# One transformer layer: memory keys started ahead of the delta-rule scans, cross attention's sums in other PSUM banks, one activation table moved

## The chip, the core and the metric

The kernel runs on one core of a Trainium2 chip. The core has a matrix engine (TensorE, PE in the profile, with its weight loads as PEld), a vector engine (VectorE, DVE), an activation engine (ScalarE, ACT), a general engine (GpSimd, POOL) and a queue engine (SyncE, SP) that issues nearly all transfers here. Matrix results land in eight PSUM banks of 128 x 512 float32. The metric is the device time of one execution in microseconds (us), the median of several runs.

## What is computed

One layer over 1024 tokens of width 1024, batch 1:

```python
h = rms_norm(x, g_mix_pre);  proj = h @ w_in           # queries, keys, values of both mixers, gates, alpha, beta
attn_o = window_attention(rope(aq), rope(ak), av)      # 8 heads, +-128 tokens
dn_o = gated_deltanet(dqkv, dgate, dalpha, dbeta)      # 4 heads, forward and backward scan over chunks
x = x + rms_norm(concat(attn_o, dn_o) @ w_out)
c = cross_attention(rms_norm(x), rms_norm(mem), w_cq, w_ckv, w_co)   # 256 memory tokens, 4 heads of 256
x = x + rms_norm(c)
f = (silu(h @ w_gate) * (h @ w_up)) @ w_down;  x = x + rms_norm(f)
```

All is float32. The kernel gets its accuracy from split operands: each operand of a dense product is stored as a rounded part `hi` and a rest `lo` (both of a faster float32 form), and a product is the three matmuls hi·hi, hi·lo and lo·hi. The split is a ScalarE cast (line 102) and a VectorE subtraction (line 103), for weights 128 x 1024 at a time.

## The kernel before

The program is written with pools of tiles, and a scheduler orders the instructions of each engine, guided by its own model of time; the source order, priorities and the pools' places decide what it may do. Each engine then runs its list strictly in that order. A tile of a pool that is closed leaves its place (in SBUF, or a PSUM bank) to the next pool on the same side, and the new tile's first writer waits for the old tile's readers.

The stages: input projections with the short convolutions and the preparation of the delta rule (to about 300 us); attention projections, the inverses' last levels (`levels`), and the window attention, which goes on in pieces (`next_windows`, two at a time) until 568 us; the two scans (`scan(0)`, `scan(1)`, each for two heads and both directions, 8 steps) interleaved with the memory's keys and values; the output projection (`mid_gemm`, tiles pmg); cross attention; its output projection; the feed-forward network.

What the change touches:

- `ORDER_3` (line 38) sets the source order of the scan stage: `M` is `memory_norm` (squares of the memory tokens into mjk and mss, scaling of mt, 16 transposes ptm, the split into mT), `s01` one step of both scans, `W` two windows, `K` one of 8 blocks of keys (`next_keys`, weights w_ckv, 24 matmuls pck of 128x256), `V` one of two halves of the values (`next_values`, 48 matmuls pcv of 128x512).
- PSUM pool `pc` with 5 banks serves the scans' products (psc) and also ptm, pck and pcv. The window attention has its 3 banks (psw/ptw and pow).
- The pool `mk` (mT and the small tiles of the memory) lies on the left side, where the tiles of `levels` were.
- `load_w` loads a weight block into one of two buffers wraw; the two memory tiles mt take the same two buffers. Its transfers, as all others, are issued by SP in the order of its list.
- The step of a scan: pk = k·S (psc), R = v − …, pv, vg and vn, the new state S, then po and pq, whose sum is the output o; from step 4 on also the output's normalisation, with transposes (line 870) and a store to `d_mix` (line 875). The output projection loads `d_mix` again (mraw, line 1067).
- `cross_attention` (line 1100 on): scores pcs in the two banks of `px`, exponentials cpr, transposes pct, the split cph/cpl, and the weighted sums pco, before in the same two banks of `px`. `cross_q` makes the queries pcq in the four banks of `pg`.
- Line 1151 runs a Silu on a small tile, so that the table of that function is loaded ahead of the feed-forward stage.

Of the kernel before, what the change touches and what calls it, by code (L numbers as in the profile page):

```python
# [10 lines left out]
F32 = mybir.dt.float32  # L11
F32R = mybir.dt.float32r
I32 = mybir.dt.int32
AF = mybir.ActivationFunctionType
ALU = mybir.AluOpType
AX = mybir.AxisListType
PSUM = bass.MemoryType.PSUM
DRAM = bass.MemoryType.DRAM

P = 128  # L20
S = 1024
D = 1024
KT = D // P
# [6 lines left out]
ML = 256  # L30
# [4 lines left out]

ORDER_1 = "D0 P0 D1 P1 D2 B0 P2 D3 P3 B1".split()
ORDER_2 = "L0 L1 G0 G1 A4 V A0 A1 L2 L3 W W W A2 A3 G2 G3 W".split()
ORDER_3 = ("M " + "s01 W K " * 5 + "s01 K " * 3 + "s01 V V").split()


_NAMES = ["ident", "mUi", "mLi", "m5", "m6", "band0", "band1", "band2", "mU", "mL", "ones"]
# [34 lines left out]
def tile_hybrid_block(  # L76
# [6 lines left out]
    nc = tc.nc  # L83
# [9 lines left out]
    def f32(ap):  # L93
        return ap.bitcast(F32)
# [13 lines left out]
    def pool(name, bufs, **kw):  # L108
        return tc.tile_pool(name=name, bufs=bufs, reuse_waits="tile", **kw)
# [42 lines left out]
    pcv = ExitStack()  # L152
# [41 lines left out]
    pg = pgs.enter_context(pool("pg", 3, space=PSUM))  # L194
# [18 lines left out]
    for hf in range(2):  # L213
        hi = hx.tile([P, KT, HALF], F32R, name=f"hhi{hf}")
        lo = hx.tile([P, KT, HALF], F32R, name=f"hlo{hf}")
        for j in range(4):
# [5 lines left out]
            ss = t1.tile([P, 1], F32, tag="ss", name="ss", bufs=4)  # L222
# [4 lines left out]
            for kq in range(2):  # L227
                pt = small()
# [15 lines left out]
    pt = small()  # L244
# [75 lines left out]
    pt = small()  # L320
# [42 lines left out]
    pt = small()  # L363
# [403 lines left out]


    p2 = ExitStack()
    pc = p2.enter_context(pool("pc", 5, space=PSUM))  # L770
    t3 = p2.enter_context(pool("t3", 2, side="right"))

    def scan(g):
# [106 lines left out]
        yield  # L880


    mk = p2.enter_context(pool("mk", 1))
    mT = [mk.tile([P, KT, ML], F32R, name=f"mT{i}") for i in range(2)]

    def memory_norm():
        mn = []
        for t in range(2):
            mt = wp.tile([P, D], F32, tag="wraw", name="mt")
            nc.sync.dma_start(mt, mem[t * P:(t + 1) * P, :])  # L890
            jk = f32(wp.tile([P, D], F32R, tag="whi", name="mjk"))
            ss = mk.tile([P, 1], F32, tag="mss", name="mss", bufs=2)
            nc.scalar.activation(jk, mt, AF.Square, accum_out=ss)
            rs = mk.tile([P, 1], F32, tag="mrs", name="mrs", bufs=2)
            rstd_of(rs, ss, 1.0 / D, EPS)
            nc.vector.tensor_scalar(mt, mt, rs, None, ALU.mult)
            mn.append(mt)
        for k2 in range(KT // 2):
            pt = pc.tile([P, 2, ML], F32, tag="pc", name="ptm")
            for i in range(2):  # L900
                k = 2 * k2 + i
                for j in range(2):
                    nc.tensor.transpose(pt[:, i, j * P:(j + 1) * P], mn[j][:, k * P:(k + 1) * P], ident)
            for i in range(2):
                k = 2 * k2 + i
                split(mT[0][:, k, :], mT[1][:, k, :], pt[:, i], gain("mem", k))
# [3 lines left out]
    def next_keys():  # L910

        ct = kv_done[0]
        kv_done[0] += 1
        whi, wlo = load_w(w_ckv[:, ct * P:(ct + 1) * P], KT, P)
        pp = pc.tile([P, 512], F32, tag="pc", name="pck")[:, 0:ML]
        for k in range(KT):
            for i, (w, a) in enumerate(((whi, 0), (whi, 1), (wlo, 0))):
                nc.tensor.matmul(pp, w[:, k, :], mT[a][:, k, :], start=(k == 0 and i == 0), stop=(k == KT - 1 and i == 2))
        cv = mk.tile([P, 512], F32, tag="cv", name="cv", bufs=2)[:, 0:ML]
        nc.scalar.copy(cv, pp)  # L920
        nc.sync.dma_start(d_mk[ct * P:(ct + 1) * P, :], cv)

    def next_values():

        ch = kv_done[1]
        kv_done[1] += 1
        pp = [pc.tile([P, 512], F32, tag="pc", name="pcv") for _ in range(2)]
        for kp in range(4):
            whi, wlo = load_w(w_ckv[kp * 256:(kp + 1) * 256, D + ch * 512:D + (ch + 1) * 512], 2, 512)
            for t in range(2):  # L930
                for kk in range(2):
                    k = 2 * kp + kk
                    for i, (w, a) in enumerate(((whi, 0), (whi, 1), (wlo, 0))):
                        nc.tensor.matmul(pp[t], mT[a][:, k, t * P:(t + 1) * P], w[:, kk, :], start=(k == 0 and i == 0),
                                         stop=(k == KT - 1 and i == 2))
        for t in range(2):
            vv = mk.tile([P, 512], F32, tag="cv", name="vv", bufs=2)
            nc.scalar.copy(vv, pp[t])
            nc.sync.dma_start(d_mv[t, :, ch * 512:(ch + 1) * 512], vv)
# [159 lines left out]
    def cross_attention(q, h):  # L1099
# [29 lines left out]
            split(ph, pl, pt)  # L1129
            pts.append((ph, pl))  # L1130
        for j in range(2):
            po = px.tile([P, 512], F32, tag="px", name="pco")
            cs = slice((2 * h + j) * P, (2 * h + j + 1) * P)
            for kt in range(2):
                for i, (a, b_) in enumerate(((0, 0), (0, 1), (1, 0))):
                    nc.tensor.matmul(po, vr_[a][:, kt, cs], pts[kt][b_], start=(kt == 0 and i == 0),  # L1136
                                     stop=(kt == 1 and i == 2))
            split(q[0][:, 2 * h + j, :], q[1][:, 2 * h + j, :], po)
# [9 lines left out]
            behind = q, h  # L1148
    q1 = q
    last = cross_attention(*behind)  # L1150
    nc.scalar.activation(last, last, AF.Silu)
    L2.close()
    Lk.close()

# [386 lines left out]
```

## Time and profile before

| | us |
|---|---|
| three runs | 1549.28, 1548.82, 1545.64 |
| median | 1548.82 |
| profiled execution | 1551.7 |
| its span, first to last instruction | 1549.9 |

| stretch of the span, us | what runs | PE busy | DVE busy | granted PE clock |
|---|---|---|---|---|
| 362.8 to 389.5 | levels' end, memory norm, first scan step | 21.82 of 26.70 | 18.57 | 0.87 |
| 389.5 to 497.2 | six scan steps, keys, windows | 102.58 of 107.70 | 95.23 | 0.98 |
| 497.2 to 533.2 | last steps, keys | 33.59 of 36.00 | 31.76 | 0.96 |
| 533.2 to 568.4 | values, windows | 32.98 of 35.20 | 22.00 | 0.94 |
| 568.4 to 640 | output projection | 71.00 of 71.60 | 42.58 | 1.00 |
| 640 to 847 | cross attention, its output projection | 207.00 of 207.00 | 96.95 | 1.00 |
| 847 to 890 | last two heads, output projection | 39.70 of 43.00 | 16.24 | 0.96 |

How to read the rows below: a row of the timeline has the start and the duration in us, the engine, the line of the kernel, the operation, output<-input tiles, shapes, how many instructions are merged (xN), and in brackets the idle time before it with what ended it. A matmul's duration includes its pipeline, so the pace of a row of matmuls is read from one start to the next. A 128x128 float32 matmul counts as two in the trace (two passes). A row of a tile's view has, after the count, the shortest, median and longest duration in ns, then the first and last start. The granted clock is 1.00 at full speed.

### The profile page before, as it was taken

The numbers are of one execution on the slowest core, as the hardware profiler recorded it, in microseconds if no ns is written. First come the engines' busy times: TensorE is split into PE (matmuls) and PEld (weight loads), VectorE is DVE, ScalarE is ACT, GpSimd is POOL, SyncE is SP. The second block draws the span as 40 slices with busy tenths as digits, with TensorE's granted clock in tenths as the row PEclk, the third lists the DMA queues.
The fourth block names the chain that finished last, engine by engine and source line by source line (L and its number), as shares of the span: only waits on it lengthen the run. The fifth ranks groups of instructions, "written<-read, shape, count | busy, mean of one in ns | idle before, by whom it ended". The sixth has DMA issues, their size and how long they took to land.

```text
span 1549.9 us, 20928 instructions
## 1 busy us (share of the span) xinstructions
PE 1494.9 (96%) x7451; PEld 1257.4 (81%) x7451; DVE 1060.1 (68%) x1762; ACT 713.3 (46%) x1377; POOL 302.6 (20%) x297
## 2 busy tenths in 40 slices
PE   6999999988999999999999999999999999999998
PEld 5888887877899878888888777888888888888786
DVE  6877898756898766443346377786868554696676
ACT  5665552236556765454334554322323332454532
POOL 2000110000003202253202231443433433000010
PEclk9999999999999999999999999999999999999999
DMA  6244456767997585354223264344433334853355
GB/s 206 74 131 124 133 150 164 209 169 246 317 305 244 161 294 173 117 181 149 69 69 130 72 205 142 112 136 129 148 119 121 102 102 147 289 189 102 109 175 165
DMA packets 267366, 247.16 MB, mean 159 GB/s; under 512 B 39016, under 2 KB 204797, under 8 KB 267261
## 3 DMA queue, kind: packets, MB, share of 16 engines
q1 hardware_dynamic: 267261, 245.82, 50.8%
q8 instruction: 59, 0.97, 0.3%
q14 instruction: 46, 0.38, 0.1%
HBM read 173.65 MB, written 69.50 MB: 157 GB/s over the span
## 4 chain that ended last, share of the span: by engine, by line
PE 80%; DMA 7%; DVE 6%; ACT 3%; SPq 2%; issue 2%; POOL 1%; DVEq 0%; ACTq 0%; POOLq 0%
PE pg L263 13%; PE pmg L1021 9%; PE pD L1212 8%; PE pE L1212 8%; PE pA L1212 7%; PE pcq L263 6%; PE pdX L1402 6%; PE pdA L1402 4%; PE pB L1212 4%; PE psc L787 2%; PE pdD L1402 2%; PE pco L1136 1%; PE pcs L1110 1%; PE pdX L1495 1%; DVE wlo L103 1%
## 5 line engine op out<-in xcount | busy, mean ns | idle before, releaser
L102 ACT CAST whi<-wraw 128x1024 fp32r<-128x1024 f32 x108 | 113.4, 1050 | 149.7 <-PE pg L263 36.0
L263 PE MATMUL pg<-hhi,whi 128*128 128x512 f32 x352 | 142.1, 405 | 2.8 <-DVE rop L732 2.8
L263 PE MATMUL pg<-hlo,whi 128*128 128x512 f32 x352 | 141.0, 401 | 0.0
L263 PE MATMUL pg<-hhi,wlo 128*128 128x512 f32 x352 | 140.7, 400 | 0.0
L103 DVE TENSOR_TENSOR wlo<-wraw,whi 128x1024 fp32r<-128x1024 f32 x78 | 95.4, 1224 | 63.4 <-ACT whi L102 62.3
L1021 PE MATMUL pmg<-whi,b 128*128 128x512 f32 x384 | 118.6, 393 | 0.2 <-ACT b L102 0.2
L1212 PE MATMUL pA<-s,whi 128*128 128x512 f32 x352 | 109.5, 392 | 1.2 <-ACT m L1229 1.0
L103 POOL TENSOR_TENSOR wlo<-wraw,whi 128x1024 fp32r<-128x1024 f32 x30 | 72.3, 2411 | 146.6 <-ACT whi L102 146.4
L1021 PEld LDWEIGHTS pmg<-whi,b 128*128 128x128 f32 x384 | 71.5, 188 | 14.7 <-ACT b L102 0.6
L263 PEld LDWEIGHTS pg<-hhi,whi 128*128 128x128 f32 x352 | 67.8, 193 | 16.9 <-DVE rop L732 3.3
L263 PEld LDWEIGHTS pg<-hhi,wlo 128*128 128x128 f32 x352 | 68.0, 193 | 13.5
L263 PEld LDWEIGHTS pg<-hlo,whi 128*128 128x128 f32 x352 | 67.9, 193 | 13.4
L1212 PEld LDWEIGHTS pA<-s,whi 128*128 128x128 f32 x352 | 65.4, 188 | 15.2 <-ACT m L1229 1.5
L1402 PE MATMUL pdX<-dhl,whi 128*128 128x512 f32 x264 | 76.1, 390 | 1.5 <-DVE zv L1457 0.8
L1021 PE MATMUL pmg<-wlo,b 128*128 128x512 f32 x192 | 72.2, 391 | 0.0
L1212 PE MATMUL pA<-s,wlo 128*128 128x512 f32 x176 | 68.6, 391 | 1.8 <-DVE wlo L103 1.8
L102 ACT CAST whi<-araw 128x1024 fp32r<-128x1024 f32 (+1 forms) x36 | 35.3, 982 | 70.8 <-PE pdX L1402 27.6
L1289 POOL TENSOR_TENSOR act<-act,up 128x512 f32<-128x512 f32 x33 | 50.1, 1519 | 88.5 <-DVE up L1288 53.2
L103 DVE TENSOR_TENSOR wlo<-araw,whi 128x1024 fp32r<-128x1024 f32 (+1 forms) x36 | 40.8, 1133 | 38.7 <-ACT whi L102 36.2
L288 DVE SCALAR_TENSOR_TENSOR acc<-cp,cols,acc 128x1024 f32<-128x1024 f32 x48 | 61.4, 1281 | 1.5 <-ACT acc L286 0.8
L1402 PEld LDWEIGHTS pdX<-dhl,whi 128*128 128x128 f32 x264 | 49.3, 188 | 12.8 <-issue 1.1
L1262 DVE TENSOR_TENSOR sr<-sr,wraw 128x512 f32<-128x512 f32 x22 | 36.6, 1662 | 28.6 <-POOL sr L1261 28.6
(410 smaller groups left out, 3963.9 us busy)
## 6 DMA issues: line engine op xcount, KB each, us to landing
wraw<-in_w_gate_up_dram SPq DMA_DIRECT2D x52, 512.0 KB, 3.9
kv<-d_kv SPq DMA_DIRECT2D x32, 512.0 KB, 6.9
wraw<-in_w_in_dram SPq DMA_DIRECT2D x22, 512.0 KB, 4.9
b<-in_w_down_dram SPq DMA_DIRECT2D x20, 512.0 KB, 7.4
araw<-d_as SPq DMA_DIRECT2D x20, 512.0 KB, 3.9
pz<-d_pz SPq DMA_DIRECT2D x32, 256.0 KB, 7.1
wraw<-in_w_ckv_dram SPq DMA_DIRECT2D x16, 512.0 KB, 7.0
wraw<-in_w_out_dram SPq DMA_DIRECT2D x16, 512.0 KB, 3.9
```

The lines of the kernel that those rows point to most:

```text
L102: nc.scalar.copy(hi, src)
L103: (eng or nc.vector).tensor_tensor(lo, src, f32(hi), ALU.subtract)
L263: nc.tensor.matmul(p_, w[:, k, :], ah[a][:, k, :], start=(k == 0 and i == 0), stop=(k == nk - 1 and i == 2))
L288: nc.vector.scalar_tensor_tensor(acc, cp[:, t:t + S], taps[t], acc, ALU.mult, ALU.add)
L787: nc.tensor.matmul(out[:, d, h, :], lt[:, d, h, :], rt[:, d, h, :], start=True, stop=True)
L1021: nc.tensor.matmul(pp[t], act[a][:, k, tt], w_[:, kk, :], start=(k == 0 and i == 0), stop=(k == KT - 1 and i == 2))
L1110: nc.tensor.matmul(pp[:, t2_, :], q[a][:, ct, tt], kr_[b_][:, ct, :], start=(j == 0 and i == 0), stop=(j == 1 and i == 2))
L1136: nc.tensor.matmul(po, vr_[a][:, kt, cs], pts[kt][b_], start=(kt == 0 and i == 0), stop=(kt == 1 and i == 2))
L1212: nc.tensor.matmul(out_, w[a][:, k, :], xx[b_][:, k, :], start=(start and k == 0 and i == 0), stop=(k == HK - 1 and i == 2), skip_group_ch ...
L1262: nc.vector.tensor_tensor(s[1], s[0], a_[:, 0:HK], ALU.subtract)
L1289: nc.gpsimd.tensor_tensor(o_, o_, up, ALU.mult)
L1402: nc.tensor.matmul(banks[t], a[:, k - k0, tt], w, start=(first and k == 0 and i == 0), stop=(k == NB - 1 and i == 2), skip_group_check=not ...
```

## The change

Three edits. First, two PSUM banks of their own (`pk`) for ptm, pck and pcv, and three instead of five for the scans; the pool `mk` is now opened ahead of the scans' tiles, at the bottom of the right side (where the normed input was), with two placeholder tiles cv in it and mss made wider; and ORDER_3 has two blocks of keys ahead of the first scan step, and none in the last three. Second, the weighted sums pco go into the four banks of `pg`. Third, the small Silu reads four columns of the last split of cross attention instead of the sums.

```diff
-ORDER_3 = ("M " + "s01 W K " * 5 + "s01 K " * 3 + "s01 V V").split()
+ORDER_3 = ("M K K " + "s01 W K " * 5 + "s01 K s01 s01 s01 V V").split()
@@
-    pc = p2.enter_context(pool("pc", 5, space=PSUM))
+    pk_ = p2.enter_context(pool("pk", 2, space=PSUM))
+    pc = p2.enter_context(pool("pc", 3, space=PSUM))
+    mk = p2.enter_context(pool("mk", 1, side="right"))
+    mT = [mk.tile([P, KT, ML], F32R, name=f"mT{i}") for i in range(2)]
+    for _ in range(2):
+        mk.tile([P, 512], F32, tag="cv", name="cv", bufs=2)
     t3 = p2.enter_context(pool("t3", 2, side="right"))
@@
-    mk = p2.enter_context(pool("mk", 1))
-    mT = [mk.tile([P, KT, ML], F32R, name=f"mT{i}") for i in range(2)]
-
     def memory_norm():
@@
-            ss = mk.tile([P, 1], F32, tag="mss", name="mss", bufs=2)
+            ss = mk.tile([P, 24], F32, tag="mss", name="mss", bufs=2)[:, 0:1]
@@
-            pt = pc.tile([P, 2, ML], F32, tag="pc", name="ptm")
+            pt = pk_.tile([P, 2, ML], F32, tag="pk", name="ptm")
@@
-        pp = pc.tile([P, 512], F32, tag="pc", name="pck")[:, 0:ML]
+        pp = pk_.tile([P, 512], F32, tag="pk", name="pck")[:, 0:ML]
@@
-        pp = [pc.tile([P, 512], F32, tag="pc", name="pcv") for _ in range(2)]
+        pp = [pk_.tile([P, 512], F32, tag="pk", name="pcv") for _ in range(2)]
@@
-            po = px.tile([P, 512], F32, tag="px", name="pco")
+            po = pg.tile([P, 512], F32, tag="pg", name="pco")
@@
-    nc.scalar.activation(last, last, AF.Silu)
+    nc.scalar.activation(last, f32(q1[0][:, KT - 1, 0:4]), AF.Silu)
```

What the scheduler makes of it differs from the first memory instructions to the output projection of cross attention; the feed-forward network's instructions stand in the same order as before.

SP's list at the first scan step. Before, all loads of the first two steps (kv, pz) stand ahead of the first key weights:

```order
L796 DMA pz<-d_pz_108 128x512
L795 DMA kv<-d_kv_103 128x1024
L796 DMA pz<-d_pz_105 128x512
L795 DMA kv<-d_kv_103 128x1024
L796 DMA pz<-d_pz_106 128x512
L795 DMA kv<-d_kv_104 128x1024
L796 DMA pz<-d_pz_107 128x512
L795 DMA kv<-d_kv_104 128x1024
L671 DMA d_mix<-ao 64x4x128
L796 DMA pz<-d_pz_108 128x512
L854 DMA gate<-d_gate 128x2x128
L127 DMA wraw<-in_w_ckv_dram 128x8x128
```

After, three weight loads stand ahead of or between them, two of them before the last stores of `levels` (d_pz):

```order
L612 DMA d_pz_108<-Z_2123 128x4x128
L127 DMA wraw<-in_w_ckv_dram 128x8x128 x2
L612 DMA d_pz_107<-Z_2122 128x4x128
L612 DMA d_pz_108<-Z_2123 128x4x128
L800 DMA kv<-d_kv_103 128x1024
L127 DMA wraw<-in_w_ckv_dram 128x8x128
L801 DMA pz<-d_pz_105 128x512
L800 DMA kv<-d_kv_103 128x1024
L801 DMA pz<-d_pz_106 128x512
L800 DMA kv<-d_kv_104 128x1024
L801 DMA pz<-d_pz_107 128x512
L800 DMA kv<-d_kv_104 128x1024
```

The first two weight loads need the buffers of the memory tiles, and the third the first one's; seven of the first step's eight loads now stand behind the third.

SP's list at the end of the scans, from the last stores of their output (osq). Before, loads of value weights stand around the loads of `d_mix`:

```order
L875 DMA d_mix<-osq 128x2x128 x2
L127 DMA wraw<-in_w_ckv_dram 128x2x512
L671 DMA d_mix<-ao 64x4x128
L875 DMA d_mix<-osq 128x2x128 x2
L995 DMA gpost<-in_g_mix_post_dram 128x1024
L1067 DMA mraw<-d_mix 128x2x512 x4
L1031 DMA xr<-in_x_dram 128x1024 x2
L127 DMA wraw<-in_w_ckv_dram 128x2x512
```

After:

```order
L671 DMA d_mix<-ao 64x4x128
L880 DMA d_mix<-osq 128x2x128 x4
L997 DMA gpost<-in_g_mix_post_dram 128x1024
L1069 DMA mraw<-d_mix 128x2x512 x4
L1033 DMA xr<-in_x_dram 128x1024 x4
L671 DMA d_mix<-ao 64x4x128
```

All value weights are loaded earlier; on PE too all 96 pcv, which stood behind the last transposes of the scans, now stand between the products from vg of the third and of the fifth scan step.

ACT's list in cross attention. Before, one head is handled between two query blocks, and the Silu (line 1151) with its table stands ahead of the last head's split (cph):

```order
L1117 ACTIVATE cpr,csum<-pcs,cmx 128x256 x4
L102 CAST whi<-wraw 128x1024 x2
L102 CAST cph<-pct 128x512 x2
L102 CAST b_7330<-pco 128x512 x2
L1117 ACTIVATE cpr,csum<-pcs,cmx 128x256 x4
L102 CAST whi<-wraw 128x1024
L1151 ACT_TABLE_LOAD
L1151 ACTIVATE csum<-csum 128x4
L102 CAST cph<-pct 128x512 x2
L102 CAST b_7330<-pco 128x512 x2
```

After:

```order
L1119 ACTIVATE cpr,csum<-pcs,cmx 128x256 x6
L102 CAST cph<-pct 128x512 x2
L1119 ACTIVATE cpr,csum<-pcs,cmx 128x256 x2
L102 CAST b_7336<-pco 128x512 x2
L102 CAST cph<-pct 128x512 x2
L102 CAST b_7336<-pco 128x512 x2
L1153 ACT_TABLE_LOAD
L1153 ACTIVATE csum<-b_7336 128x4
L102 CAST whi<-wraw 128x1024 x3
```

The scores of two heads now follow each other (eight exponentials around one split), all heads are done before the output projection starts, and the table stands behind the last split.

## The prediction

> **What bounds the kernel now.** First the page's busy times, then the busy time of each engine by stretch (start and end, length, then busy time of PE, PEld, DVE, ACT, POOL, granted clock, DMA share, GB/s):
>
> ```profile
> PE 1494.9 (96%) x7451; PEld 1257.4 (81%) x7451; DVE 1060.1 (68%) x1762; ACT 713.3 (46%) x1377; POOL 302.6 (20%) x297
> ...
> 362.80:389.50 26.70, 21.82 (x136) 18.46 (x134) 18.57 (x52) 19.25 (x46) 2.34 (x6) 0.87 0.70 239
> 389.50:497.20 107.70, 102.58 (x796) 97.40 (x796) 95.23 (x265) 63.53 (x173) 13.24 (x21) 0.98 0.92 284
> 497.20:533.20 36.00, 33.59 (x247) 31.31 (x246) 31.76 (x87) 24.49 (x78) 11.33 (x14) 0.96 0.56 171
> 533.20:568.40 35.20, 32.98 (x153) 26.51 (x151) 22.00 (x38) 27.07 (x51) 1.25 (x2) 0.94 0.84 285
> ...
> 640.00:847.00 207.00, 207.00 (x1044) 175.20 (x1043) 96.95 (x147) 95.21 (x184) 57.15 (x48) 1.00 0.35 115
> 847.00:890.00 43.00, 39.70 (x199) 32.18 (x198) 16.24 (x24) 23.63 (x47) 10.19 (x8) 0.96 0.22 75
> ```
>
> TensorE sets the time nearly everywhere. No matmul is removed, so the change can only win or lose TensorE's idle time and the slow time behind an idle gap. From 362.8 to 568.4 the idle time is 4.9 + 5.1 + 2.4 + 2.2 = 14.6 us. The slow time shows in the starts behind a gap:
>
> ```profile
> 333.31 0.79 PE L263 MATMUL pg<-hhi,whi 128*128 128x512 f32 x1 [2.83 <-DVE rop L732]
> 333.90 0.63 PE L263 MATMUL pg<-hlo,whi 128*128 128x512 f32 x1
> 334.33 0.63 PE L263 MATMUL pg<-hhi,wlo 128*128 128x512 f32 x1
> ...
> 339.45 0.40 PE L263 MATMUL pg<-hhi,wlo 128*128 128x512 f32 x1
> 339.69 0.40 PE L263 MATMUL pg<-hhi,whi 128*128 128x512 f32 x1
> ```
>
> For 6.1 us the same matmul starts every 0.43 us instead of 0.23: 14 matmuls, 2.8 us lost beside the 2.83 us of the gap. A long gap is paid about twice. In the scans VectorE is nearly as full as TensorE (95.23 of 107.70).
>
> **TensorE's work, moved.** The order of both programs says how many matmuls stand between two marks; their pace (start to start) is here:
>
> ```profile
> 405.52 0.40 PE L918 MATMUL pck<-mT,whi 128*128 128x256 f32 x2
> ...
> 405.88 0.40 PE L918 MATMUL pck<-mT,whi 128*128 128x256 f32 x2
> ...
> 473.90 1.95 PE L787 MATMUL psc<-S,kv 128*128 128x128 f32 x16
> 475.68 0.83 PE L787 MATMUL psc<-kv,pz 128*128 128x128 f32 x6
> ...
> 536.27 0.62 PE L934 MATMUL pcv<-whi,mT 128*128 128x512 f32 x2
> 536.72 0.39 PE L934 MATMUL pcv<-wlo,mT 128*128 128x512 f32 x1
> ```
>
> So 0.12 us for a pck (three in 0.36), 0.228 for a pcv, 0.22 for a scan product (8 in 1.78): a block of keys is 24 x 0.12 = 2.9, both halves of the values 96 x 0.228 = 21.9, a full scan step 40 x 0.22 = 8.9, and the window pieces fill the rest. Counted so, in us of work from the last projection matmul to the first output-projection matmul, cut at the first product from vg of each step and at the scans' last transposes:
>
> | | to step 1 | six steps | last steps | to pmg | sum |
> |---|---|---|---|---|---|
> | before | 15.0 | 16.5 16.0 15.8 17.0 15.7 16.3 = 97.3 | 31.4 | 30.2 | 173.9 |
> | after | 23.4 | 19.3 21.7 25.8 24.1 12.3 15.5 = 118.7 | 23.9 | 4.2 | 170.2 |
>
> 3.7 us of window pieces come behind the first pmg instead. The question is what each cell takes on the clock.
>
> **To step 1: +8.3 us (0 to +13).** Rows of the memory's tiles, of the levels, and of the first scan load:
>
> ```profile
> L890 SPq DMA_DIRECT2D mt<-in_mem_dram x2: 432/444/457, 344.7 to 345.2; - x2
> L893 ACT ACTIVATE mjk<-mt x2: 1048/1054/1059, 378.4 to 379.5; 128x1024 f32<-128x1024 f32 x2
> L896 DVE TENSOR_SCALAR mt<-mt,mrs x2: 747/750/754, 380.5 to 382.0; 128x1024 f32<-128x1024 f32 x2
> ...
> 365.02 0.27 ACT L598 ACTIVATE z<-ps 128x128 f32<-128x128 f32 x1
> ...
> 366.93 1.07 PE L587 MATMUL ps<-mov,L 128*128 128x64 f32 x8 [0.24 <-ACT Z L606]
> ...
> 375.87 0.62 SPq L795 DMA_DIRECT2D kv<-d_kv  x1
> ...
> wraw<-in_w_ckv_dram SPq DMA_DIRECT2D x16, 512.0 KB, 7.0
> ...
> L103 DVE TENSOR_TENSOR wlo<-wraw,whi 128x1024 fp32r<-128x1024 f32 x78 | 95.4, 1224 | 63.4 <-ACT whi L102 62.3
> ```
>
> The memory is in SBUF long before 365, so the early norm can start. But its two squares now stand ahead of z on ScalarE (2 x 1.05 = 2.1 us), its scalings ahead of and between the levels' copies on VectorE (2 x 0.75), and 8 of its transposes ahead of the levels' products on PE. Added up with the copies that wait in turn, I put ps<-mov at 371.5 instead of 366.93, the levels' stores 4.5 us later, and the memory's last transpose at 378. Only then can the first key weights be issued; SP waits there, and the two last d_pz stores and all scan loads wait behind it. At the third weight load SP waits again, until the first block is landed and split: 378.5 + 4 to 7 (7.0 is the group's median) + 1.05 + 1.22 = 385 to 388. Seven of the eight loads of step 1 follow it, a load of kv or pz takes as long to land as the weights, so step 1 begins at about 394 instead of 384, less what it now has done (the keys, 7.4 us of work, run from 385 on): the mark 389.5 moves to 397 or 398. Lower bound 0: the 23.4 us of work fit the 26.70 if no load is late. Upper bound: 395 + 7.
>
> **Six steps: +21.2 us (+14 to +27).** The first four hold 90.9 us of TensorE work; the five settled steps before needed 85.4 us of time (107.7 less the first's 22.3) for 80.8 of work, so 96.1. The fifth and sixth have 12.3 and 15.5 of TensorE work, but VectorE's scan and window work stays: 95.23 / 6 = 15.9 us a step, less one weight split (1.2) at most. Between full (14.7) and its occupancy of before (15.9 / 0.88 = 18) I take 16.4 each, 32.8. Together 128.9 against 107.7.
>
> **Last steps: -4.5 us (-7 to 0).** The keys leave (5.8 of TensorE, two splits of VectorE), so VectorE sets it: 31.76 less 2 x 1.2 and some window pieces, 28.4, at 0.9 occupancy 31.5 against 36.0.
>
> **To the output projection: -21.2 us (-23 to -18).** The values, which covered the way of the scans' output through `d_mix`, are gone from here:
>
> ```profile
> 532.20 1.06 PE L870 MATMUL psc<-ident,ol 128*128 128x128 f32 x4
> 568.43 0.73 PE L1021 MATMUL pmg<-whi,s 128*128 128x512 f32 x2
> ...
> L1067 SPq DMA_DIRECT2D mraw<-d_mix x4: 390/460/721, 535.8 to 537.3; - x4
> L102 ACT CAST s<-mraw x4: 1054/1058/1061, 542.7 to 546.0; 128x1024 fp32r<-128x1024 f32 x4
> ...
> DMA to landing us min/median/max: 7.4/7.8/8.2
> ```
>
> The way itself: transposes end 533.2, mraw issued at 535.8 (2.6), landed 7.4 later, cast 1.05: 11.1, taken as 11.5, with 4.2 us of work to fill it. So the 35.2 us become 11.5, and a gap of 7 us adds the 2.5 to 2.8 us of slow matmuls behind it: 14. What is late next is nothing: the output projection has its weights early. The 3.7 us of window pieces are added behind.
>
> The Trainium skill ("TensorE: Matmul & The Clock Gate", "What's actually happening") has the half clock come only after an idle window of about 3.4 us and last about 3.4 us of work. The row above has it after 2.83 us of idling and for 6.1 us; by the page the gap here would cost 1.7 instead of 2.5, and the sum would be 0.8 lower.
>
> **Cross attention and its tail: -0.3 us (-5 to +4).**
>
> ```profile
> 768.32 3.04 PE L1110 MATMUL pcs<-kr,b 128*128 128x256 f32 x24
> ...
> 769.95 0.69 DVE L1112 TENSOR_REDUCE cmx<-pcs 128x2 f32<-128x512 f32 x1 [1.65 <-PE pcs L1110]
> ...
> 771.40 0.46 ACT L1117 ACTIVATE cpr<-pcs,cmx 128x256 f32<-128x256 f32 x1
> ...
> 849.41 0.73 PE L1136 MATMUL pco<-cph,vr 128*128 128x512 f32 x2 [0.56 <-ACT cph L102]
> 850.78 0.50 PE L1136 MATMUL pco<-cpl,vr 128*128 128x512 f32 x1 [0.64 <-DVE cpl L103]
> ...
> 863.14 1.28 ACT L1151 ACT_TABLE_LOAD   x1
> 864.43 0.20 ACT L1151 ACTIVATE csum<-csum 128x4 f32<-128x4 f32 x1
> ...
> 865.16 1.22 PE L1136 MATMUL pco<-cph,vr 128*128 128x512 f32 x2 [1.49 <-ACT cph L102]
> ```
>
> The tail lost 3.3 us of idling (43.0 - 39.7) and 1.7 of clock (0.96 of 43). The table, 1.28 + 0.2, is the wait of 1.49; moved behind, that gap goes. But the scores of two heads now follow each other in two banks. A half's bank is free 2.1 us after its last score (769.8 to 771.9), the next half but one wants it 12 x 0.12 = 1.45 later: 0.6 us of waiting a pair, and 0.3 where pco follows pct with no query between. Three pairs x 0.9 = 2.7; the last pair, which has nothing between, 0.6 + 0.3 and waits like the 0.56 and 0.64 above, 2.0. So 4.7 new against 5.0 gone. At -5 the pair waits are hidden; at +4 the gains fail to come.
>
> The Trainium skill ("ScalarE: Activation LUTs", "What ACT_TABLE_LOAD costs") counts 1.28 us for the load and 1.38 for a drain. Here the Silu starts 0.01 us behind the load, with no drain between; by the page 2.7 us would leave that wait, and the sum would be 1.2 lower.
>
> **The sum:** 8.3 + 21.2 - 4.5 - 21.2 + 3.7 - 0.3 = +7.2 us, on 1551.7 for the profiled execution 1558.9. The three runs have their median 2.9 lower (1548.8): **1556**.
>
> **The rivals.** (1) The front fills as it is written: the loads are in time, the mark stays at 389.5, and the sum is -1.1: 1547.7. For it: 4.9 us idle there and 0.87 of clock, room for two blocks of keys. Against: SP's two waits ahead of the scan's own loads. (2) Faster: the front fills, the six steps run at 0.97 of TensorE (118.7 / 0.97 = 122.4, +14.7), and the pairs' waits are hidden (-5): 0 + 14.7 - 4.5 - 21.2 + 3.7 - 5 = -12.3, 1536.5. For it: three of the settled steps run with TensorE full. Against: the late steps have 12.3 and 15.5 of work and VectorE's 15.9. It decides if the six steps take under 124 us. (3) Three banks are too few: a step uses six banks a head group, and the next step's pk wants one that the sum of po and pq frees, four VectorE additions of 0.68; if 2.7 us of that are on the path in seven steps, +19 on the forecast: 1575. Against: before, waits of psc for VectorE were under 1 us each.
>
> **How the numbers follow.** Forecast 0.45 (1556, its own range 1549 to 1564), rival 1 0.27, rival 2 0.18, rival 3 0.10. A difference of 0.3% (4.6 us) is about what a measurement tells from none. Slower by more: 0.39 of the forecast and all of rival 3, rounded up 0.50; within: 0.06 of the forecast and 0.22 of rival 1, 0.28; faster: rival 2 and the rest of rival 1, 0.22. The range leaves out half of rivals 2 and 3: 1540 to 1570.
>
> **What would show it.** The stretch from the last projection matmul to the first product from vg: 35 us if SP's waits are real, 27 if not; on SP, the third weight load waiting for a split. Six steps: 129 us, the last two near 16 with TensorE under 0.9 busy. From the last transposes to pmg: 11 to 12 us with 7 idle and a slow clock behind. Cross attention: short waits of pct and pco in each pair, none at the table. I am wrong if the loads of step 1 land by 389, if the late steps take under 14 us, or if the output projection starts within 8 us of the scans' end.

## The result, and where the time went

The changed kernel takes 1573.59 us (median of four runs, 1571.66 to 1577.64) against 1547.23 for the kernel before: a ratio of 1.0174 with a 95% interval of 1.0153 to 1.0194, so 26 us slower. The forecast was slower too, but 1556 us, and its range ended at 1570. The profiled execution of the changed kernel took 1572.7 us against 1551.7, its span is 1570.9 against 1549.9: 21.0 us have to be found in the two traces.

First the page's busy times of the kernel after, then its busy times by stretch, cut at the marks that the prediction used (last projection matmul, first product from vg of the first and of the seventh step, the scans' last transposes, first pmg) and then at 640, 690 and 830 us up to the feed-forward network. The columns are start and end, length, busy time of PE, PEld, DVE, ACT and POOL, granted clock, DMA share and GB/s.

```profile
PE 1494.9 (95%) x7451; PEld 1257.7 (80%) x7451; DVE 1060.8 (68%) x1762; ACT 713.8 (45%) x1377; POOL 304.1 (19%) x297
```

```profile
358.80:402.00 43.20, 32.32 (x202) 28.38 (x201) 26.17 (x66) 27.00 (x61) 2.34 (x6) 0.88 0.68 209
402.00:527.40 125.40, 121.78 (x881) 112.65 (x880) 102.47 (x267) 69.28 (x176) 13.23 (x21) 1.00 0.87 284
527.40:556.40 29.00, 25.92 (x194) 23.26 (x194) 27.53 (x80) 21.59 (x72) 11.40 (x15) 1.00 0.47 130
556.40:566.00 9.60, 6.89 (x32) 5.26 (x30) 5.39 (x18) 8.45 (x19) 0.30 (x2) 0.76 0.85 251
566.00:640.00 74.00, 74.00 (x333) 61.21 (x332) 49.20 (x53) 43.53 (x75) 12.91 (x16) 0.98 0.59 208
640.00:690.00 50.00, 49.43 (x252) 41.34 (x250) 22.58 (x26) 28.78 (x44) 24.11 (x22) 1.00 0.51 168
690.00:830.00 140.00, 122.96 (x621) 104.30 (x622) 59.46 (x112) 52.63 (x122) 23.91 (x10) 0.95 0.22 68
830.00:921.40 91.40, 91.40 (x420) 75.88 (x419) 37.15 (x40) 41.52 (x73) 24.54 (x29) 1.00 0.40 132
```

TensorE is busy for the same 1494.9 us as before (slow matmuls count as busy), so in sum the loss is idle time. Against the stretches of before, in us:

| stretch | before | after | change | forecast |
|---|---|---|---|---|
| to the last projection matmul | 362.8 | 358.8 | -4.0 | 0 |
| to step 1 | 26.7 | 43.2 | +16.5 | +8.3 |
| six scan steps | 107.7 | 125.4 | +17.7 | +21.2 |
| last steps | 36.0 | 29.0 | -7.0 | -4.5 |
| to the output projection | 35.2 | 9.6 | -25.6 | -21.2 |
| output projection and cross attention | 332.4 | 355.4 | +23.0 | +3.4 |
| feed-forward network | 649.1 | 649.5 | +0.4 | 0 |

The first line is chance: the instructions there are the same, and in the runs below the mark lies anywhere between 358 and 363. The scan stage, which the forecast was about, gained and lost nearly what it should in sum. The one line that is wrong by 20 us is the one that the forecast put at next to nothing: cross attention, where from 690 to 830 us TensorE now idles for 17.0 us and runs at a granted clock of 0.95.

The view of waits for that stretch, then the timeline of one pair of heads in the kernel after (rows on TensorE, VectorE, GpSimd and ScalarE that belong to the wait):

```profile
PE pcs L1112 <- ACT cpr L1119: 14.2, 4, 6.2
```

```profile
773.49 2.07 PE L1112 MATMUL pcs<-kr,b 128*128 128x256 f32 x16
...
774.63 2.36 POOL L103 TENSOR_TENSOR wlo<-wraw,whi 128x1024 fp32r<-128x1024 f32 x1 [3.04 <-ACT whi L102]
774.64 0.69 DVE L1114 TENSOR_REDUCE cmx<-pcs 128x2 f32<-128x512 f32 x1 [4.32 <-PE pcs L1112]
775.25 0.68 DVE L103 TENSOR_TENSOR b<-pcq,b 128x512 fp32r<-128x512 f32 x1
775.85 1.17 DVE L1115 TENSOR_SCALAR cmx<-cmx 128x2 f32<-128x2 f32 x1
...
777.58 0.46 ACT L1119 ACTIVATE cpr<-pcs,cmx 128x256 f32<-128x256 f32 x1
...
778.18 3.14 PE L1112 MATMUL pcs<-kr,b 128*128 128x256 f32 x24 [2.62 <-ACT cpr L1119]
```

This is one of four waits of TensorE for the exponentials, 14.2 us in all. Eight of the head's 24 scores stand earlier, among the query products. Of the 16 here the first eight complete the head's first half: VectorE, idle until then, starts its maximum 1.15 us after the first of the 16, and before it started 1.63 us after the first of twelve (769.95 and 768.32), which is four scores of 0.12 us more. The other eight are the second half, and the next product is already the next head's, which wants the first half's bank. That bank is free when its second exponential ends, at 777.58 + 0.46 = 778.04: 3.6 us after its last score (773.49 + 8 x 0.12 = 774.45), where the prediction had read 2.1. The 1.5 us more lie between the maximum (774.64) and the end of its scaling: VectorE's list has the split of a query block between the two (0.5), and the scaling itself takes 1.17 instead of 0.17 (1.0). And only eight scores, 1.0 us, cover the way, where the prediction counted twelve, 1.45. So the wait is 2.62 instead of the 0.6 of the forecast, and three pairs have one of 2.62 to 2.75 (in the last of them a split of weights stands in VectorE's list instead of the slow scaling).

The first pair waits 6.2 us. In its timeline ScalarE stands at a transfer, the weights of the next norm (gpost), ahead of that pair's exponentials:

```profile
691.36 0.34 SPq L997 DMA_DIRECT2D gpost<-in_g_cross_post_dram  x1
...
695.85 1.06 ACT L998 ACTIVATE gpost<-gpost 128x1024 f32<-128x1024 f32 x1 [3.47 <-DMA gpost<-in_g_cross_post_dram]
696.81 0.46 ACT L1119 ACTIVATE cpr<-pcs,cmx 128x256 f32<-128x256 f32 x1
...
697.87 4.42 PE L1112 MATMUL pcs<-kr,b 128*128 128x256 f32 x22 [6.21 <-ACT cpr L1119]
```

The slow clock follows three of these four waits: the 22 scores behind the 6.21 us take 4.42 us, where 24 took 3.04 in the kernel before. The granted clock, read around the four waits:

```profile
694.51:701.34 6.83, 3.47 (x16) 3.48 (x17) 2.23 (x5) 2.88 (x9) 0.00 (x0) 0.50 0.80 317
735.47:738.89 3.42, 0.99 (x8) 0.99 (x9) 2.98 (x7) 1.94 (x8) 1.24 (x1) 1.00 0.27 82
738.89:742.30 3.41, 3.41 (x18) 3.41 (x18) 1.62 (x4) 1.02 (x4) 0.00 (x0) 0.50 0.24 71
776.43:779.84 3.41, 1.66 (x14) 1.66 (x14) 2.94 (x7) 1.94 (x8) 0.56 (x1) 1.00 0.47 140
779.84:783.26 3.42, 2.91 (x23) 2.60 (x22) 2.77 (x8) 2.21 (x7) 0.00 (x0) 1.00 0.08 21
817.39:820.81 3.42, 3.42 (x18) 3.42 (x18) 2.31 (x5) 0.58 (x4) 0.00 (x0) 0.50 0.25 96
```

TensorE works for 3.47 + 3.41 + 3.42 = 10.3 us at half the clock, so the clock costs about 5.1 us beside the 17.0 us of idling; before, cross attention lost 3.3 us idle and 1.7 of clock, all at its tail. 17.0 + 5.1 - 5.0 is 17 of the 23 us. The window pieces that stand behind the first pmg now (3.7 us by the forecast's count) are most of the rest.

In the scan stage, the order of events at the front, SP's rows of the kernel after (a wait of SP shows as a hole between its rows), then the view of SP's waits:

```profile
376.80 1.38 SPq L127 DMA_DIRECT2D wraw<-in_w_ckv_dram  x2
378.28 2.67 SPq L612 DMA_DIRECT2D d_pz<-Z  x2
384.91 0.34 SPq L800 DMA_DIRECT2D kv<-d_kv  x1
385.35 0.38 SPq L127 DMA_DIRECT2D wraw<-in_w_ckv_dram  x1
...
392.35 0.32 SPq L801 DMA_DIRECT2D pz<-d_pz  x1
```

```profile
SPq L800 <- DMA d_pz<-Z: 3.8, 2, 3.2
...
SPq L801 <- DMA wraw<-in_w_ckv_dram: 1.6, 1, 1.6
```

The first load of a scan step goes out at 384.9, 26 us behind the last projection matmul, where the kernel before had it 13 us behind (375.87 and 362.8). It waits 3.2 us for the levels' last store to land: the scans' tiles have moved up behind the memory's, onto places that this store still reads. That is read from the order of the pools; the run with the old place, below, has no such wait. Behind it SP stands 1.6 us more, until a weight load has landed, before the first step's last pz goes out (392.35).

### The profile page after: what moved, and what is told of

It reads as the page before. It is cut to its first block, busy times and chain, and to the rows that moved or that the text cites. A ratio compares the mean times of both kernels' runs of the same rounds, so it can differ in the third digit from the quotient of the medians.

```text
span 1570.9 us, 20950 instructions
## 1 busy us (share of the span) xinstructions
PE 1494.9 (95%) x7451; PEld 1257.7 (80%) x7451; DVE 1060.8 (68%) x1762; ACT 713.8 (45%) x1377; POOL 304.1 (19%) x297
## 4 chain that ended last, share of the span: by engine, by line
PE 82%; DVE 6%; DMA 6%; ACT 2%; issue 2%; SPq 1%; POOL 0%; DVEq 0%; POOLq 0%; ACTq 0%
PE pg L263 13%; PE pmg L1023 11%; PE pD L1214 7%; PE pE L1214 7%; PE pA L1214 7%; PE pcq L263 6%; PE pdX L1404 5%; PE pdA L1404 4%; PE pB L1214 4%; PE psc L792 3%; PE pdX L1497 2%; PE pdD L1404 2%; PE pcs L1112 2%; PE pco L1138 1%; PE pcv L936 1%
## 5 line engine op out<-in xcount | busy, mean ns | idle before, releaser
L1023 PE MATMUL pmg<-whi,b 128*128 128x512 f32 x384 | 115.0, 391 | 0.0
```

Source lines behind the costliest of these rows:

```text
L1023: nc.tensor.matmul(pp[t], act[a][:, k, tt], w_[:, kk, :], start=(k == 0 and i == 0), stop=(k == KT - 1 and i == 2))
```

## The experiments

**The three edits apart.** The first edit alone (the memory's place, the two banks, ORDER_3):

```diff
+ORDER_3 = ("M K K " + "s01 W K " * 5 + "s01 K s01 s01 s01 V V").split()
+    pk_ = p2.enter_context(pool("pk", 2, space=PSUM))
+    pc = p2.enter_context(pool("pc", 3, space=PSUM))
+    mk = p2.enter_context(pool("mk", 1, side="right"))
```

> The change's first edit alone (two banks pk, memory tiles at the bottom of the right side, keys ahead in ORDER_3); cross attention and the small Silu as before. By the forecast's terms: 8.3 + 21.2 - 4.5 - 21.2 + 3.7 = +7.5 us, a ratio of about 1.005. By the marks in the trace of after (front +16.6, six steps +17.6, last steps -6.5, to the output projection -26.1, and 3.7 us of window pieces behind it): +5.3 us, 1.0034. If the scans carry the whole loss of 26 us: 1.017.

Measured: 1.0048 (1.0032 to 1.0064), +7.4 us. The second edit alone:

```diff
-            po = px.tile([P, 512], F32, tag="px", name="pco")
+            po = pg.tile([P, 512], F32, tag="pg", name="pco")
```

> The change's second edit alone: the sums pco in the four banks of pg, all else as before, the small Silu at its old place. By the forecast's terms: pair waits of 4.7 us against 3.5 us of the tail gone, so 0 to +4 us, at most 1.003. By the reading of the two traces, where the stretch from the first output-projection matmul to the feed-forward network grew by 23.0 us, 3.7 of them window pieces: +18 to +21 us, 1.012 to 1.014, with the four waits of pcs for cpr (6.2, 2.6, 2.6, 2.7 us) in its trace.

Measured: 1.0154 (1.0138 to 1.0170), +24 us, and in its trace the same waits, with one of 2.04 us at the table, whose Silu still stands ahead of the last split:

```profile
734.99 4.64 PE L1110 MATMUL pcs<-kr,b 128*128 128x256 f32 x24 [2.63 <-ACT cpr L1117]
...
827.14 0.73 PE L1136 MATMUL pco<-cph,vr 128*128 128x512 f32 x2 [2.04 <-ACT cph L102]
```

The third edit alone:

```diff
-    nc.scalar.activation(last, last, AF.Silu)
+    nc.scalar.activation(last, f32(q1[0][:, KT - 1, 0:4]), AF.Silu)
```

> The change's third edit alone: the small Silu reads the last split. If the wait of 1.49 us at the table is the whole price, with the slow clock behind it: -1.5 to -3.2 us, ratio 0.998 to 0.999. If something else ends late there in its place: no change, 1.000.

Measured: 0.9996 (0.9984 to 1.0008). The trace has the wait go from 1.49 to 0.46 us, and the stretch from the first pmg to the feed-forward network at 330.0 us instead of 332.4:

```profile
863.60 0.73 PE L1136 MATMUL pco<-cph,vr 128*128 128x512 f32 x2 [0.46 <-ACT cph L102]
```

The times can't tell such a gain from none. So nearly the whole loss is the second edit's. The three alone add up to 0.48 + 1.54 - 0.04 = 1.98% against 1.74% for the change, each uncertain by 0.12 to 0.2, so they add up within the noise. The Silu may be worth a little more beside the second edit, where it removes a wait of 2.04 instead of 1.49; the times don't show it.

**Why the pairs wait.** If VectorE's steps hold the bank, an exponential that needs none of them sets it free at once. This kernel is the second edit with the maximum of the softmax left out, so one step of the computation is missing, and TensorE's list keeps the pairs:

```diff
-            nc.vector.tensor_reduce(mxs[:, 2 * tp:2 * tp + 2], pp, axis=AX.X, op=ALU.max)
-            nc.vector.tensor_scalar(mxs[:, 2 * tp:2 * tp + 2], mxs[:, 2 * tp:2 * tp + 2], -1.0 / 16.0, None, ALU.mult)
...
-                nc.scalar.activation(pr[:, t2_, :], pp[:, t2_, :], AF.Exp, bias=mxs[:, n:n + 1], scale=1.0 / 16.0,
+                nc.scalar.activation(pr[:, t2_, :], pp[:, t2_, :], AF.Exp, scale=1.0 / 16.0,
```

> The second edit alone, with the maximum taken out of cross attention's softmax (no reduction and no scaling of it on VectorE; the exponentials start from the scores): TensorE's list keeps the heads in pairs. If the pairs wait because a bank of scores comes free only behind VectorE's steps (maximum, then a split of the queries, then the scaling: 4.2 us and more instead of 2.1): the three waits of pcs of 2.6 us fall to 0 to 0.6 us and the slow clock behind them goes, the first wait, of ScalarE for gpost, stays: 8 to 11 us less than the second edit alone, a ratio of 1.008 to 1.011. If the pairs cost by themselves (transposes and sums that wait for the next step of the same head): the waits move to pct or pco, and 1.013 or more.

Measured: 1.0029 (1.0013 to 1.0046): 19 of the 24 us are gone, more than expected. (By the rows above a bank is held for 3.6 us, not 4.2.) The waits of the three later pairs fall to 0.27, and the scores behind them run at full pace; the first falls to 1.51, which was not expected (the exponentials now stand ahead of gpost's transfer on ScalarE):

```profile
690.03 3.14 PE L1110 MATMUL pcs<-kr,b 128*128 128x256 f32 x24 [1.51 <-ACT cpr L1115]
...
726.62 3.14 PE L1110 MATMUL pcs<-kr,b 128*128 128x256 f32 x24 [0.27 <-ACT cpr L1115]
```

The waits do not move to the transposes, and pco's are 0.5 to 0.7. So the later pairs cost next to nothing by themselves; what costs is the bank that VectorE's steps hold. The run doesn't part the split in VectorE's list from the slow scaling, and some of its 19 us are the first pair's, which the next run shows.

The part of gpost was tried by itself, in the second edit alone:

```diff
-        nc.scalar.mul(t, t, math.sqrt(D))
+        if pool_scale:
+            nc.gpsimd.tensor_scalar(t, t, math.sqrt(D), None, ALU.mult)
+        else:
+            nc.scalar.mul(t, t, math.sqrt(D))
...
-    gp = gpost_tile(tz, g_cross_post)
+    gp = gpost_tile(tz, g_cross_post, pool_scale=True)
```

> The second edit alone, and the weights of the next norm (gpost of cross attention) scaled on GpSimd instead of ScalarE; TensorE's list stays but for two products. If the first wait of pcs for cpr (6.97 us in the run of the second edit alone) is ScalarE standing at gpost's transfer ahead of the exponentials: it falls to the 2.6 to 3.5 us of the other pairs, with the slow clock behind it -4 to -6 us against that run, a ratio to before of 1.0115 to 1.013. If the exponentials are late for another reason: 1.015.

Measured: 1.0127 (1.0110 to 1.0144), 4 us less than the second edit alone, and the first wait is 3.03 instead of 6.97:

```profile
693.68 4.96 PE L1113 MATMUL pcs<-kr,b 128*128 128x256 f32 x22 [3.03 <-ACT cpr L1120]
```

**The exchange the other way round.** Before, with the scores in the four banks and the sums alone in the two:

```diff
-            pp = px.tile([P, 2, ML], F32, tag="px", name="pcs")
+            pp = pg.tile([P, 2, ML], F32, tag="pg", name="pcs")
```

> Before, with the scores pcs in the four banks of pg and the sums pco alone in the two banks of px: the exchange the other way round. If the loss comes from two heads' scores that follow each other in two banks, this has no such waits: the stretch from 680 to 847 stays without idle time and the last two heads have the output projection between their steps, -2 to -5 us, 0.997 to 0.999. If any arrangement that parts scores and sums makes the heads run in pairs with waits: +5 us or more, over 1.003.

Measured: 0.9976 (0.9961 to 0.9990), 3.7 us faster. In TensorE's list a head's scores now have 17 to 29 products of queries or of the output projection behind them before its transposes, and the trace has one wait for the exponentials, of 0.93 us:

```profile
PE pcs L1110 <- ACT cpr L1117: 0.9, 1, 0.9
```

The tail that lost 3.3 us of idling before is full (50.00 of 50.00 us from 847 to 897), since both last heads' steps have the output projection between them. It is a change of order as well as of banks, so it shows what the exchange is worth here, not what a bank is worth.

**Inside the first edit.** Its parts were undone one by one, with the second and third edit left out. Five shared banks again, the place and ORDER_3 as changed:

```diff
-    pk_ = p2.enter_context(pool("pk", 2, space=PSUM))
-    pc = p2.enter_context(pool("pc", 3, space=PSUM))
+    pc = p2.enter_context(pool("pc", 5, space=PSUM))
```

> The first edit with one part undone: five banks shared by scans, keys and values as before, the memory tiles still at the bottom of the right side and ORDER_3 as changed. Work of TensorE by the list, in us: 24.3 to step 1, 93.8 in six steps, 25.6 in the last, 30.2 to the output projection (the values are back there). If the place makes the front late: to step 1 still 40 to 45 us instead of 27 to 32, six steps 100 to 105, last steps 30, to the output projection 36: +2 to +9 us, 1.001 to 1.006. If the front was late by the two banks of their own: to step 1 under 34 us, and -6 to 0 us in all, 0.996 to 1.000.

Measured: 1.0144 (1.0129 to 1.0160), +22 us. The front is late (46 us to step 1, 40 to 45 expected), the six steps (101) and the last (32) came about as expected; but to the output projection it takes 44 us instead of 36, for a reason that was not expected. ScalarE's list has the cast of the second half's operand (b), whose transfer goes out 32 us behind that of the first half (mraw, 545.5), ahead of the four casts of the first half's. On SP, ScalarE and TensorE:

```profile
577.35 0.42 SPq L1068 DMA_DIRECT2D b<-d_mix  x1
...
582.80 1.04 ACT L102 CAST b<-b 128x1024 fp32r<-128x1024 f32 x1 [4.05 <-DMA b<-d_mix]
```

```profile
584.85 2.50 PE L1022 MATMUL pmg<-whi,s 128*128 128x512 f32 x5 [9.61 <-ACT s L102]
```

The memory's tiles at their old place, the banks and ORDER_3 as changed:

```diff
-    mk = p2.enter_context(pool("mk", 1, side="right"))
+    mk = p2.enter_context(pool("mk", 1))
```

(the second line behind the scans' tiles, where it was).

> The first edit with the other part undone: memory tiles on the left side as before, banks and ORDER_3 as changed. On SP the scans' loads stand ahead of all key weights again. Work by the list: 13.0 to step 1, 128.8 in six steps, 25.0 in the last, 4.4 to the output projection. If the place makes the front late: to step 1 back at 27 to 32 us; six steps 131 to 135, last 28 to 30, to the output projection 10: -4 to +3 us, 0.997 to 1.002. If the banks do: to step 1 over 38 us, and +8 us or more, over 1.005.

Measured: 0.9995 (0.9982 to 1.0007), and 25 us to step 1. SP's rows have the first load right behind the last store, 13 us behind the last projection matmul (374.1 and 361.1) instead of 26, with all key weights behind the first steps' loads:

```profile
372.91 0.56 SPq L612 DMA_DIRECT2D d_pz<-Z  x1
...
374.14 0.77 SPq L796 DMA_DIRECT2D kv<-d_kv  x1
```

So with the two banks of their own the place makes the front late: 44 us with the new one, 25 with the old. With five shared banks it is late at the new place (46), and the last run of this series will show it as late at the old. Places and banks as changed, ORDER_3 as before:

```diff
-ORDER_3 = ("M K K " + "s01 W K " * 5 + "s01 K s01 s01 s01 V V").split()
+ORDER_3 = ("M " + "s01 W K " * 5 + "s01 K " * 3 + "s01 V V").split()
```

> The first edit with ORDER_3 as before: places and banks changed, no keys asked for ahead of the first step. The scheduler still puts 46 products of keys there; the third weight load stands behind the first step's loads, not among them. If SP's wait at the third load makes step 1 late (the forecast had 6 to 9 us from it): to step 1 35 to 38 us instead of 44, and 1.000 to 1.002 in all. If the front is late already by the memory's work ahead of the levels, and by the loads that wait for the place: to step 1 41 to 45 us, 1.004 to 1.006.

Measured: 1.0079 (1.0057 to 1.0102), a little above what was expected, and 43 us to step 1. The third weight load stands behind the first step's loads here, and the front is as late all the same; SP's wait at that load was not what made it late. ORDER_3 alone, with places and banks as before:

```diff
-ORDER_3 = ("M " + "s01 W K " * 5 + "s01 K " * 3 + "s01 V V").split()
+ORDER_3 = ("M K K " + "s01 W K " * 5 + "s01 K s01 s01 s01 V V").split()
```

> Only ORDER_3 as changed (two blocks of keys asked for ahead of the first step, none in the last three), places and five shared banks as before. TensorE's list has 48 products of keys ahead of the first step; SP's list has their weights behind 15 of the 16 loads of the first two steps. So step 1 waits on TensorE behind keys whose weights land last: weights issued at 389, landed at 396, split by 398 to 400, keys to 403: to step 1 42 to 47 us instead of 27 to 32, six steps 100 to 104, last 30, to the output projection 33 to 36; +2 to +10 us, 1.001 to 1.006. If the keys fill only time that was idle there: to step 1 28 to 34 us and 0.994 to 0.998.

Measured: 1.0048 (1.0031 to 1.0065), and 49 us to step 1 (42 to 47 expected): the keys stand ahead of it on TensorE, and their weights land behind 15 loads of the scans. The first key product starts at 395.93, 37 us behind the last projection matmul. So a late front has two causes here, each enough alone: the new place, or keys ahead of the step in shared banks.

All runs by the same stretches, from the starts in their traces, in us (the scans' last transposes count from their start here, under 1 us ahead of the mark above):

| kernel | to step 1 | six steps | last | to pmg | pmg to feed-forward |
|---|---|---|---|---|---|
| before | 27 | 107 | 35 | 36 | 332 |
| after | 44 | 125 | 28 | 10 | 356 |
| first edit | 44 | 126 | 28 | 10 | 335 |
| second edit | 26 | 107 | 35 | 36 | 358 |
| second, gpost on GpSimd | 28 | 109 | 35 | 37 | 351 |
| second, no maximum | 28 | 106 | 36 | 37 | 337 |
| third edit | 26 | 109 | 35 | 37 | 330 |
| scores in pg | 32 | 105 | 36 | 36 | 329 |
| place new, banks old | 46 | 101 | 32 | 44 | 334 |
| place old, banks new | 25 | 132 | 31 | 13 | 335 |
| place and banks new, ORDER_3 old | 43 | 128 | 30 | 12 | 333 |
| ORDER_3 alone | 49 | 100 | 28 | 35 | 333 |

The kernels whose scan stage is that of before (six of these) differ by 6 us at the front with the same instructions; a difference below that says nothing there.

**A kernel that is faster than both.** Own banks with the memory's tiles at their old place, ORDER_3 as changed, and the scores in pg (against the kernel before):

```diff
-ORDER_3 = ("M " + "s01 W K " * 5 + "s01 K " * 3 + "s01 V V").split()
+ORDER_3 = ("M K K " + "s01 W K " * 5 + "s01 K s01 s01 s01 V V").split()
...
+    pk_ = p2.enter_context(pool("pk", 2, space=PSUM))
+    pc = p2.enter_context(pool("pc", 3, space=PSUM))
...
+            pp = pg.tile([P, 2, ML], F32, tag="pg", name="pcs")
```

> Two parts that cost nothing or gain, together: own banks for keys and values with the memory's tiles at their old place (0.9995 alone), and scores in pg with the sums alone in px (0.9976 alone). If they add: 0.996 to 0.998, and faster than both kernels compared before. If the bank order of the one spoils the other: 0.999 or more.

Measured: 0.9954 (0.9937 to 0.9971), 1540.65 us, 7 us faster than the kernel before and 33 faster than the changed one. That is a little better than the two gains together (0.9995 x 0.9976 = 0.9971), but within the interval. Its stretches, and TensorE's longest wait in the last of them:

```profile
358.90:384.60 25.70, 19.81 (x119) 16.91 (x118) 16.71 (x46) 16.84 (x39) 2.16 (x5) 0.87 0.73 229
384.60:516.20 131.60, 130.49 (x963) 122.25 (x963) 111.86 (x286) 78.56 (x198) 13.47 (x22) 1.00 0.92 293
...
546.90:559.80 12.90, 7.12 (x37) 5.06 (x36) 7.07 (x19) 11.95 (x29) 0.20 (x1) 0.85 0.82 271
```

```profile
557.78 0.79 PE L666 MATMUL pow<-ph,vhl 128*128 128x512 f32 x1 [3.98 <-ACT ph L102]
```

With keys and values in the six steps TensorE is full there (130.49 of 131.60). What it loses is the uncovered way through `d_mix`, 12.90 us with 7.12 of work; 3.98 of it TensorE waits for a window piece whose split stands in ScalarE's list behind the scaling of gpost, as the first pair did in cross attention. So the values were held back behind the scans again, as a cover:

```diff
-                        nc.tensor.matmul(pp[t], mT[a][:, k, t * P:(t + 1) * P], w[:, kk, :], start=(k == 0 and i == 0),
+                        m_ = nc.tensor.matmul(pp[t], mT[a][:, k, t * P:(t + 1) * P], w[:, kk, :], start=(k == 0 and i == 0),
...
+                        if ch == 0 and kp + t + kk + i == 0:
+                            tc.keep_in_program_order(m_)
```

> The fastest kernel so far (own banks, old place, scores in pg) with all 96 products of the values held back behind the scans, where they cover the way of the scans' output through d_mix as before the change. Work by the list: 13.0 to step 1, 106.9 in six steps, 24.5 in the last, 29.6 to the output projection. If the covered way is worth only what the late steps lose by it (VectorE sets two of them at 16 to 17 us instead of 21 and 23 of TensorE's work): to step 1 25 to 26, six steps 112 to 116, last 30, to the output projection 33 to 36, 1 to 4 us slower than without, a ratio to before of 0.996 to 0.998. If the idle way with its slow clock costs more than the late steps gain: 0.992 to 0.994.

Measured: 0.9971 (0.9957 to 0.9985), as expected, with its interval across that of the kernel without. The six steps take 111.7 us and the way to pmg 37.1, 148.8 together against 144.5. The covered way still idles for 4.1 us (37.10 - 33.01) against 5.8 without cover, and the six steps for 2.1 instead of 1.1: the cover gains nothing that the times show.

```profile
385.20:496.90 111.70, 109.62 (x867) 104.47 (x867) 100.59 (x278) 67.03 (x182) 14.18 (x22) 1.00 0.95 294
...
526.20:563.30 37.10, 33.01 (x152) 26.09 (x151) 23.12 (x39) 27.48 (x51) 2.39 (x2) 0.95 0.83 282
```

## Why the prediction was wrong

**The step that failed** is "Cross attention and its tail: -0.3 us (-5 to +4)", and in it the term for the pairs, 4.7 us. The mechanism was named (the scores of two heads in two banks) and its size was wrong, in three ways. The time in which a bank comes free was read where the scores of one head stood alone: 2.1 us, with twelve scores to cover it. In a pair VectorE's list has other work between the maximum and its scaling, the scaling is slow, and the 2.1 became 3.6, with eight scores to cover it; 2.62 us of waiting instead of 0.6. The sum counted the waits at their own length, though the prediction had itself found that a gap of 2.83 us is paid about twice; with waits of 2.6 us and more the slow clock took another 5.1. And the first pair was not looked at: before, by TensorE's list, 83 query products stood between the first head's scores and its transposes and covered ScalarE's wait for gpost, and now the next head's scores follow behind 16 transposes; 6.21 us. In the kernel before:

```profile
703.95 1.06 ACT L996 ACTIVATE gpost<-gpost 128x1024 f32<-128x1024 f32 x1 [1.88 <-DMA gpost<-in_g_cross_post_dram]
```

The pairs' term of 4.7 so became 14.2 us of waiting and 5.1 of clock. The gain of the tail came in part: its waits went from 3.3 us to 1.2 (0.28, 0.42 and 0.54).

**The scan stage** was right in its sum by luck, since its terms were wrong both ways. The first edit alone was forecast at +7.5 us and measured at 1.0048, +7.4. To step 1 it was +16.5 instead of +8.3, and beyond the upper bound of 13. The levels' products (ps<-mov) started 11 us behind the last projection matmul instead of 4.1, 7 us later where 4.5 was forecast. VectorE's list has the scaling of mt ahead of the levels' copies, and VectorE stood idle there until GpSimd had the factor mrs, which waits for ScalarE's squares:

```profile
362.90 0.75 DVE L898 TENSOR_SCALAR mt<-mt,mrs 128x1024 f32<-128x1024 f32 x1 [3.69 <-POOL mrs L164]
...
369.77 2.13 PE L587 MATMUL ps<-mov,L 128*128 128x64 f32 x16
```

Then the first load of the scans came later still, by the 3.2 us for the place, which the forecast did not have; and SP's 1.6 us at a weight load's landing. The forecast laid the delay on SP's wait at the third weight load; in the trace SP goes on there at once (384.91, then 385.35), and the run with that load behind the others is as late. How the 16.5 us divide over these was read from the trace and not tried apart. Against that, the six steps took 17.7 instead of 21.2 (their last two 13.8 and 17.1 us, forecast at 16.4 each, so one of them under the 14 us that the prediction had named as a sign of being wrong), the last -7.0 instead of -4.5, and the way to pmg -25.6 instead of -21.2: there mraw landed in 6.1 us instead of 7.8, and the window pieces, slow as they ran, left a gap of 2.7 us instead of 7:

```profile
L1069 SPq DMA_DIRECT2D mraw<-d_mix x4: 360/464/697, 559.2 to 560.6; - x4
...
DMA to landing us min/median/max: 5.7/6.1/6.6
```

**The rivals.** The time came nearest to rival 3 (1575), but its mechanism is not in the trace: the waits of psc in the six steps are 1.6 us in all against 1.8 before, and with three banks and the old place the six steps run 128.8 us of work (by the list) in 132. Rival 1 (the front fills, the loads are in time) is what the kernel with the old place does, with the keys later and not in front. Rival 2's bound of 124 us for the six steps was missed by 1.4. That no rival had cross attention as the loss is the fault of the list: one was owed to every term that was the difference of two larger ones.

## What to carry to other kernels

A bank is free when the last reader behind it is done, and that reader stands in a list with other work: read the delay from the list as it will be, not from a place in the old trace where the engine had nothing else to do. A term that is small because a gain and a loss nearly cancel (4.7 against 5.0) has the uncertainty of both, and a wait that is long enough for the clock to fall counts for more than its length (here 17.0 us of idling brought 5.1 of slow clock). And a place in SBUF carries a wait like a bank does: where a pool is moved, the tiles that slide with it wait for other readers.

## What the runs showed of the hardware

The scaling of two columns (128 x 2) on VectorE took 0.17 us, but 1.17 in two of the pairs: there GpSimd's split of a weight block ran from 774.63 for 2.36 us, and the scaling ended at 777.02, 0.03 us behind it. In the third pair GpSimd was idle and the same instruction took 0.16:

```profile
815.78 0.16 DVE L1115 TENSOR_SCALAR cmx<-cmx 128x2 f32<-128x2 f32 x1
```

So a small VectorE instruction on SBUF can stand for the rest of a long one on GpSimd; the maximum and the split beside it, which read PSUM, ran at their usual 0.69 and 0.68. The Trainium skill ("Trainium Architecture — The Big Picture", "What this means for kernel authors") says that VectorE and GpSimd share one pair of SBUF ports and that the sharing is a lock, not a division of bandwidth; this trace agrees.

The slow clock does not follow from the length of a wait alone. Behind the pair's wait of 2.62 us above, 24 scores took 3.14 us, which is full pace; behind the pair before it, with 2.63 us, they took 4.64; and in the run with gpost on GpSimd they took 3.15 behind 2.63 (at 734.25). The row of the pair before:

```profile
737.90 4.64 PE L1112 MATMUL pcs<-kr,b 128*128 128x256 f32 x24 [2.63 <-ACT cpr L1119]
```

What differs is how the wait lies on a grid of 3.41 us. In the changed kernel's trace the stretches at half the clock begin at 694.51, 738.89 and 817.39, and the distances are 13 and 23 times 3.41, however the waits lie. By the rows of the granted clock above, the piece of the grid ahead of 738.89 has 2.43 us without a matmul (3.42 - 0.99), and half the clock follows; the wait of the same length at 775.56 is cut by the grid at 776.43, its second piece has 1.75 us without one (3.41 - 1.66), and full clock follows. Between 1.75 and 2.43 these rows set no border.
